# One decoder block with 32 experts on one core: the expert stage's tensor engine in written order, its gather and scatter products between weight chunks, and the first biases as three bfloat16 parts

## Chip, core and metric

The kernel runs on one NeuronCore of a Trainium2 chip. The metric is the device time of one execution in microseconds (us). Five engines work side by side: PE (TensorE: products and transposes, into PSUM), DVE (VectorE), ACT (ScalarE), POOL (GpSimd) and SP (SyncE, which here only issues transfers). PEld is PE's loading of the stationary operand. Sixteen DMA engines move data from HBM to the on-chip memory. A float32 product is recorded as two instructions, so a count in the trace is twice the count in the program for these.

## What is computed

A decoder block on 256 tokens of 1024 channels: a recurrent branch and an attention branch, merged and projected, a layer norm, and then a mixture of 32 experts of which each token uses 4, and a second layer norm. The change concerns the experts:

```python
def moe_ffn(x, router_w, router_b, expert_w_in, expert_b_in, expert_w_out, expert_b_out):
    ...
    logits = (xf @ router_w + router_b).astype(jnp.float32)
    top_val, top_idx = lax.top_k(logits, TOP_K)
    weights = jax.nn.softmax(top_val, axis=-1)
    ...
        h = xf[toks] @ expert_w_in[e] + expert_b_in[e]
        gate_h = jnp.minimum(h[:, :D_EXPERT], SWIGLU_LIMIT)
        lin_h = jnp.clip(h[:, D_EXPERT:], -SWIGLU_LIMIT, SWIGLU_LIMIT)
        act = gate_h * jax.nn.sigmoid(SWIGLU_ALPHA * gate_h) * (lin_h + 1.0)
        return act @ expert_w_out[e] + expert_b_out[e]
    ...
    out = jax.ops.segment_sum(ys * row_w[:, None].astype(ys.dtype), row_tok, num_segments=n_tok)
```

`expert_w_in[e]` is 1024 x 2048 and `expert_w_out[e]` 1024 x 1024, both float32: 12 MiB for each expert.

## The kernel before

The first part (branches, merge, projection, first norm, router) ends with `xg`, the rows of the first two experts' tokens. Everything after it is the expert stage. An expert has 64 slots (`CAP`) for its tokens. Experts go in pairs; a pair's 128 slots are filled together.

The weights come in 384 chunks of 1 MiB, twelve for each expert: eight for the first product (one for each 128 input channels) and four for the second. `stream` (line 770) issues their transfers from SP in the order of use, through `fetch`; they land in 21 places that are used in turn (`slots`, line 751: most are tiles named `ring`, some are pairs of halves named `wr`, `wh`/`wl`). A chunk can only be fetched into a place once PE has used the chunk that was there 21 chunks earlier.

The loop over `steps` (line 1365) writes for each expert e: `hidden` (products `h`, line 1254, after the bias products on line 1246), `swiglu` (DVE and ACT make `lc` out of `h`), `down` of expert e-1 (products `y`, line 1284), and `turned` (line 1273: `lc` transposed into `at`, which the next `down` reads). For each pair there are besides: `places` (DVE: the 0/1 matrix `oh` of the pair), `gather` (16 products `t<-oh,x`, line 1089, and eight evacuations by ACT and DVE into `xg`, line 1092), `weighted` and `scatter_weights` (two transposes of `oh`, line 1235, into `ct`), and `combine` (four products `t<-yp,ct`, line 1293, that DVE adds to `acc`, line 1297). `residual` and `spread` add the residual and the second biases, once each. Products of 64 slots use half of the array's columns, and the two halves of an expert's columns go one after the other on the two halves of the array.

Ahead of the expert stage a helper `queued` (line 122) fixes each engine's order as written. In the expert stage PE's instructions do not go through it: there the framework's scheduler sets the order, from its own estimates. The bias products of an expert take `expert_b_in` as float32 half rows on 64 partitions (`bin_`, the first 64 rows of the tile `biases`), with two columns of the identity as stationary operand; four products for each expert.

Before expert 16 stands `overflow()` (line 1299): each engine reads the largest number of tokens of an expert and branches; only if it is above 64 a slow loop runs, and in this data it does not. SP has then issued the first 21 chunks of expert 16 and what follows it.

Of the kernel before, what the change touches and what calls it, by code (L numbers as in the profile page):

```python
# [18 lines left out]
P = 128  # L19
# [15 lines left out]
# estimates, in us, of how long a step's other engines take before the tensor engine can go on with it:  # L35
# only the order in which work is traced rests on them
# [25 lines left out]
def shape_constants():  # L62
# [19 lines left out]
    # below the diagonal the level at which the two tokens' blocks merge; -0.5 on it, -1 above  # L82
# [15 lines left out]
def together(inputs):  # L98
    """small parameters, as rows of P of one array"""
# [12 lines left out]
def hybrid_block_kernel(ctx: ExitStack, tc: tile.TileContext, A, out):  # L112
# [5 lines left out]
    # instructions of one engine that follow each other as traced  # L118
# [17 lines left out]
    # slots of the experts' weights that hold other data first  # L136
# [8 lines left out]
    # halves of chunks: raw, and in two parts  # L145
# [30 lines left out]
    # the tensor engine's clock is up when the first data comes  # L176
# [6 lines left out]
    # ---- first loads  # L183
# [8 lines left out]
    def split(raw, n, engine):  # L192
        """hi and lo parts of half a chunk, rounded to float32r"""
# [24 lines left out]
    # the first products' data in small pieces  # L218
# [4 lines left out]
    # ---- small parameters  # L223
# [25 lines left out]
    # ---- the tensor engine's work, in the order in which it is traced  # L249
# [14 lines left out]
    # ---- x, with the channels on the partitions, in two parts  # L264
# [34 lines left out]
    def vectors():  # L299
# [4 lines left out]
        # sigmoid(z) is (1 + tanh(z / 2)) / 2, in the table that holds exp  # L304
# [7 lines left out]
    def three(ps, a, b, first, last, same_first=True):  # L312
        """ps += a^T b with a = (hi, lo), b = (hi, lo)."""
# [14 lines left out]
    def gemm_tm(w, ps, i):  # L328
        """[128 tokens, 2 blocks, 256 columns]"""
# [7 lines left out]
    # products of x with chunks of w_in: those that are asked for, else a gate's  # L337
# [40 lines left out]
    def shifted(ps, col, dst):  # L378
        """token shift: dst [128, 2, 256]."""
# [6 lines left out]
    # ---- low-rank inputs  # L386
# [13 lines left out]
    def rwkv_half(hf):  # L400
# [1111 lines left out]
```

## Time and profile before

| | us |
|---|---|
| median of 3 runs | 1300.01 (1298.52 to 1303.08) |
| span of the profiled execution | 1300.0 |
| expert stage (first `h` product to the end) | 299.6 to 1300.0 |

| engine | busy in the profiled execution |
|---|---|
| PE | 1225.3 us, 94% |
| DVE | 396.6 us, 31% |
| ACT | 263.2 us, 20% |
| POOL | 80.9 us, 6% |
| 16 DMA engines, main queue | 85.1% of their time |

The span leaves nothing of the time out, so sums can be made against it as it is. Busy shares are averages over stages of different kinds; the expert stage is read by stretches, and by who waits for whom. Matmul ends are modelled, so a PE that is shown busy is not PE at its peak: starts of groups are the better measure.

### The profile page before, as it was taken

What the parts mean: (1) busy time and instruction counts of PE and PEld (TensorE: products, weight loads), DVE (VectorE), ACT (ScalarE), POOL (GpSimd) and SP (SyncE); (2) the same over time, 40 slices, a digit from 0 to 9 for tenths busy, and PEclk for the clock granted to TensorE, in tenths of its full rate; (3) what the DMA queues carried; (4) which work ended last, traced back from release to release, by engine and by line L of the source; (5) the groups of instructions that cost most, each with busy time, mean ns of one, the idle gap of its engine ahead of it and who ended that gap; (6) DMA issues with size and microseconds to landing.
All of it is one profiled execution on the core that took longest, in us unless ns stands there. A gap on an engine that the chain in (4) does not pass through costs nothing. (4 is left out here: it accounts for less than half of the span.)

```text
span 1300.0 us, 15918 instructions
## 1 busy us (share of the span) xinstructions
PE 1225.3 (94%) x6524; PEld 593.2 (46%) x6524; DVE 396.6 (31%) x762; ACT 263.2 (20%) x486; POOL 80.9 (6%) x58
## 2 busy tenths in 40 slices
PE   9889989999999999999999998999999899999996
PEld 7778888974334332333323323334332323333433
DVE  6976762762123322111212201211112111111023
ACT  7456435542101010101101100101010101010111
POOL 2321221330000000000000000000000000000001
PEclk9989999999999999999999998999999999998899
DMA  8432442979999999999999997999999999999820
GB/s 271 147 102 95 176 163 101 327 275 376 412 416 413 415 415 415 412 405 410 406 413 373 412 417 318 410 418 414 414 416 413 416 412 416 416 415 403 339 97 33
DMA packets 114500, 439.32 MB, mean 338 GB/s; under 512 B 10062, under 2 KB 38552, under 8 KB 89592
## 3 DMA queue, kind: packets, MB, share of 16 engines
q1 hardware_dynamic: 113992, 437.94, 85.1%
q8 instruction: 53, 0.87, 0.3%
q10 hardware_dynamic: 432, 0.33, 0.1%
q14 instruction: 23, 0.19, 0.0%
HBM read 437.18 MB, written 1.05 MB: 337 GB/s over the span
## 5 line engine op out<-in xcount | busy, mean ns | idle before, releaser
L1254 PE MATMUL h<-ring,xg 128*64 128x512 f32 x1552 | 349.9, 598 | 0.0
L1254 PEld LDWEIGHTS h<-ring,xg 128*64 128x64 f32 x1552 | 108.7, 137 | 220.2 <-issue 209.6
L1284 PE MATMUL y<-ring,at 128*64 128x512 f32 x768 | 187.0, 619 | 1.9 <-ACT at L1275 1.9
L1262 DVE TENSOR_SCALAR h<-h 128x512 f32<-128x512 f32 x32 | 22.4, 699 | 399.6 <-PE h L1254 375.5
L1263 ACT ACTIVATE lc<-h 128x512 f32<-128x512 f32 x32 | 19.1, 597 | 492.7 <-DVE h L1262 433.0
L1246 PE MATMUL h<-biases,ident 64*64 64x512 f32 x256 | 93.1, 627 | 18.7 <-DVE lc L1266 13.3
L1284 PEld LDWEIGHTS y<-ring,at 128*64 128x64 f32 x768 | 53.6, 140 | 110.9 <-issue 103.5
L124 PE MATMUL g<-xh,wh 128*128 128x256 f32 x304 | 94.1, 310 | 2.6 <-DVE ring L384 1.9
L124 PE MATMUL g<-xh,wl 128*128 128x256 f32 x304 | 86.3, 284 | 1.5 <-DVE wl L199 1.5
L124 PE MATMUL g<-xl,wh 128*128 128x256 f32 x304 | 86.1, 283 | 0.0
L1297 DVE TENSOR_TENSOR acc<-acc,t 128x512 f32<-128x512 f32 x56 | 38.5, 687 | 140.8 <-PE t L1293 140.8
L1286 ACT COPY yp<-y 64x512 f32<-64x512 f32 x62 | 35.9, 579 | 210.6 <-PE y L1284 210.1
L1089 PEld LDWEIGHTS t<-oh,x 128*128 128x128 f32 x480 | 59.1, 197 | 26.0 <-issue 26.0
L124 POOL TENSOR_TENSOR acc<-acc,x 128x256 f32<-128x256 f32 x4 | 3.9, 994 | 1013.2 <-DVE ln_rs L124 1013.0
L1089 PE MATMUL t<-oh,x 128*128 128x128 f32 x480 | 66.2, 288 | 0.0
L124 PEld LDWEIGHTS g<-xh,wh 128*128 128x128 f32 x304 | 58.3, 192 | 11.9 <-issue 7.8
L1293 PE MATMUL t<-yp,ct 128*128 128x512 f32 x120 | 55.5, 605 | 6.8 <-ACT yp L1286 6.8
L124 PEld LDWEIGHTS g<-xl,wh 128*128 128x128 f32 x304 | 58.3, 192 | 2.2 <-issue 2.2
L124 PEld LDWEIGHTS g<-xh,wl 128*128 128x128 f32 x304 | 58.1, 191 | 1.9 <-DVE wl L199 1.7
L1092 DVE TENSOR_SCALAR xg<-t,gbc 128x128 f32<-128x128 f32 x60 | 24.6, 410 | 112.7 <-ACT xg L1092 112.7
L1246 PEld LDWEIGHTS h<-biases,ident 64*64 64x64 f32 x256 | 19.6, 135 | 76.2 <-issue 68.3
L1254 PE MATMUL h<-wr,xg 128*64 128x512 f32 x224 | 53.7, 597 | 0.0
(379 smaller groups left out, 1320.7 us busy)
## 6 DMA issues: line engine op xcount, KB each, us to landing
ring<-in_expert_w_in_dram SPq DMA_DIRECT2D x194, 1024.0 KB, 12.9
ring<-in_expert_w_out_dram SPq DMA_DIRECT2D x99, 1024.0 KB, 11.4
wr<-in_expert_w_in_dram SPq DMA_DIRECT2D x56, 512.0 KB, 13.5
wr<-in_w_in_dram SPq DMA_DIRECT2D x40, 512.0 KB, 3.8
wh<-in_expert_w_in_dram SPq DMA_DIRECT2D x34, 512.0 KB, 11.4
wl<-in_expert_w_in_dram SPq DMA_DIRECT2D x34, 512.0 KB, 11.4
wh<-in_expert_w_out_dram SPq DMA_DIRECT2D x20, 512.0 KB, 10.3
wl<-in_expert_w_out_dram SPq DMA_DIRECT2D x20, 512.0 KB, 10.2
```

The source lines that it names most:

```text
L124: queues[e] = make(*a, **k)
L1089: last = nc.tensor.matmul(ps[:, i * ns:(i + 1) * ns], lhsT=x1[:, b, k * P:(k + 1) * P], rhs=oh[:, b, :], start=b == 0 and i == 0, stop=b = ...
L1092: def scaled(ps, n, k0, put=lambda e, make, **a: make(**a)):
L1246: nc.tensor.matmul(h[half * CAP:(half + 1) * CAP, q, :], lhsT=sel_e[:, q:q + 1].to_broadcast([2 * E, CAP]), rhs=bin_[:, half * 512:(half + ...
L1254: nc.tensor.matmul(h[half * CAP:(half + 1) * CAP, q, :], lhsT=xg[:, k, sl], rhs=wi(k, c0), start=not early_bias and k == 0, stop=early_bia ...
L1262: nc.vector.tensor_scalar(out=gate_, in0=gate_, scalar1=7.0, scalar2=None, op0=ALU.min)
L1263: nc.scalar.activation(out=lc, in_=gate_, func=AF.Sigmoid, scale=1.702)
L1284: nc.tensor.matmul(y[dh * CAP:(dh + 1) * CAP, :], lhsT=at[:, kf % 4, kf // 4, :], rhs=wo_(kf, dh), start=kf == 0, stop=kf == KD - 1)
L1286: nc.scalar.copy(out=yp[r0_:r0_ + CAP, dh * 512:(dh + 1) * 512], in_=y[dh * CAP:(dh + 1) * CAP, :])
L1293: nc.tensor.matmul(ps, lhsT=ct[0:ns, b, :], rhs=yp[0:ns, hs], start=True, stop=True)
L1297: nc.vector.tensor_tensor(out=acc[:, b, hs], in0=acc[:, b, hs], in1=ps, op=ALU.add)
```

## The change

It does these things.

- **Order.** In the expert stage PE's instructions go through a wrapper `pe`, which is `queued("pe", ...)` except inside the overflow loop: PE runs them as written.
- **Where a pair's side work is written.** `gather` of the next pair comes whole after the odd expert's `hidden`, ahead of the `down` of the expert before. `combine` of a pair comes inside the `hidden` of the next pair's odd expert, after its second chunk. The transposes of `oh` come after the fourth chunk of the odd expert's `hidden`, `residual` in three pieces inside the `hidden` of experts 4 and 6, the four `spread` of the second norm inside that of expert 30.
- **First biases.** `expert_b_in` is fetched three times (32 rows each) by POOL into the memory of `acc`; DVE (first 1024 columns) and POOL (the others) split it into three bfloat16 parts that add up to the float32 value, on 96 partitions. A bias product then has one bfloat16 column of `own_rows` as stationary operand, and still there are four for each expert. The fetch of the float32 biases by SP ahead of the stage is gone.
- The transposed second-bias weights (`wtt`) live in the router's weights `rw` instead of a `ct`, and the second `started` pieces move by two chunks.

The diff, cut to its core (comment lines and renamed sites alike in kind are left out):

```diff
-    bin_ = biases[0:2 * E, :]
+    bin_ = biases[0:3 * E, :].bitcast(BF16)
...
+    own_rows = pers.tile([3 * E, E], BF16, name="own_rows")
+    for q in range(3):
+        qs = slice(q * E, (q + 1) * E)
+        nc.gpsimd.tensor_copy(out=own_rows[qs], in_=ident[qs, qs])
...
-            fetch(out=bin_, in_=L("expert_b_in").rearrange("e (h c) -> (e h) c", h=2))
...
+    raw_b = acc.rearrange("p b d -> p (b d)")[0:3 * E]
+    for q in range(3):
+        nc.gpsimd.dma_start(out=raw_b[q * E:(q + 1) * E], in_=L("expert_b_in"))
+    for eng, hs in ((nc.vector, slice(0, F)), (nc.gpsimd, slice(F, 2 * F))):
+        eng.tensor_copy(out=bin_[:, hs], in_=raw_b[:, hs])
+        for n in (2 * E, E):
+            eng.tensor_tensor(out=raw_b[0:n, hs], in0=raw_b[0:n, hs], in1=bin_[0:n, hs], op=ALU.subtract)
+            eng.tensor_copy(out=bin_[0:n, hs], in_=raw_b[0:n, hs])
+    free_order = [False]
+
+    def pe(make, *a, **k):
+
+        return make(*a, **k) if free_order[0] else queued("pe", make, *a, **k)
...
-                    nc.tensor.matmul(h[half * CAP:(half + 1) * CAP, q, :], lhsT=sel_e[:, q:q + 1].to_broadcast([2 * E, CAP]), rhs=bin_[:, half * 512:(half + 1) * 512], start=first, stop=not first)
+                    c0 = q * F + half * 512
+                    pe(nc.tensor.matmul, h[half * CAP:(half + 1) * CAP, q, :], lhsT=row.to_broadcast([3 * E, CAP]), rhs=bin_[:, c0:c0 + 512], start=first, stop=not first)
...
-                    nc.tensor.matmul(h[half * CAP:(half + 1) * CAP, q, :], lhsT=xg[:, k, sl], rhs=wi(k, c0), start=not early_bias and k == 0, stop=early_bias and k == KD - 1)
+                    pe(nc.tensor.matmul, h[half * CAP:(half + 1) * CAP, q, :], lhsT=xg[:, k, sl], rhs=wi(k, c0), start=not early_bias and k == 0, stop=early_bias and k == KD - 1)
+            for what in between.get(k, ()):
+                what()
...
+    extra = {}
+
+    def during(e, k, what):
+        extra.setdefault(e, {}).setdefault(k, []).append(what)
...
+    def gathered_(p):
+        p.xg = gather(p.oh, 2) if p.n else xg_t
+        p.ohw = weighted(p.oh, wt[:, :, 2 * p.n:2 * p.n + 2], 2) if p.n else None
...
+    for n, p in enumerate(pairs_of):
+        p.n = n
+        during(2 * n + 1, 3, lambda p=p: turned_weights(p))
+        if n < E // 2 - 1 and 2 * n + 2 != E // 2:
+            during(2 * n + 3, 1, lambda p=p: combined(p))
+            during(2 * n + 1, 3, lambda p=pairs_of[n + 1]: placed(p))
+    for j in range(2):
+        r = residual(j)
+        for k in (4, 5, 7):
+            during(4 + 2 * j, k, lambda r=r: next(r, None))
+    during(0, 5, softmax)
...
+            h = hidden(p.xg, slice(i * CAP, (i + 1) * CAP), lambda k, c0: part(c[k], c0, 512), own_rows[:, e:e + 1], e > 1, extra.get(e, {}))
+            if i and e < E - 1 and e + 1 != E // 2:
+                gathered_(pairs_of[e // 2 + 1])
             lc = swiglu(h)
```

PE around experts 8 to 10, before: expert 9's `h`, then expert 8's `y`. (`t<-ident,lc` is `turned`, `t<-oh,x` a gather, `t<-ident,oh` the transposes of `oh`, `t<-yp,ct` a combine.)

```order
L1254 MATMUL h<-ring,xg 64x512 x8
L1235 MATMUL t<-ident,oh 128x128 x2
L1254 MATMUL h<-ring,xg 64x512 x24
L1284 MATMUL y<-ring,at 64x512 x4
L1273 MATMUL t<-ident,lc 128x128 x4
L1089 MATMUL t<-oh,x_121 128x128 x2
L1284 MATMUL y<-ring,at 64x512 x4
L1089 MATMUL t<-oh,x_121 128x128 x6
```

The same place after the change (line 124 is `queued`):

```order
L124 MATMUL h<-ring,xg 64x512 x8
L124 MATMUL t<-yp,ct 128x512 x4
L124 MATMUL h<-ring,xg 64x512 x8
L124 MATMUL t<-ident,oh 128x128 x2
L124 MATMUL h<-ring,xg 64x512 x16
L1094 MATMUL t<-oh,x_121 128x128 x16
L124 MATMUL y<-ring,at 64x512 x16
L124 MATMUL t<-ident,lc 128x128 x4
L124 LDWEIGHTS own_rows
L124 MATMUL h<-biases,own_rows 64x512
```

`turned` of expert 9 stood after a quarter of expert 8's `y`, and now stands after all of it; the gather stood in pieces inside `y` and now stands whole ahead of it; the combine of the pair before moved in between the chunks of expert 9.

PE at the start of the stage, before (expert 0's last products, its biases, then expert 1):

```order
L1254 MATMUL h<-ring,xg 64x512 x32
L1246 MATMUL h<-biases,ident 64x512 x4
L1216 LDWEIGHTS ones
L1216 MATMUL t<-mk,ones 128x32
L1216 LDWEIGHTS ones
L1216 MATMUL t<-mk,ones 128x32
L1254 MATMUL h<-ring,xg 64x512 x11
L1273 MATMUL t<-ident,lc 128x128 x4
```

After, from the last of expert 0's four bias products on:

```order
L124 LDWEIGHTS own_rows
L124 MATMUL h<-biases,own_rows 64x512
L124 MATMUL t<-ident,lc 128x128 x4
L124 MATMUL h<-ring,xg 64x512 x16
L124 MATMUL t<-ident,oh 128x128 x2
```

`turned` of expert 0 moved ahead of all products of expert 1.

DVE at the same place, before, from the last `weighted` of the first pair to expert 0's `swiglu`:

```order
L1163 TENSOR_TENSOR oh<-oh,wt 128x128
L1262 TENSOR_SCALAR h<-h 128x512
L1217 TENSOR_REDUCE cnt<-t 1x1
L1218 CAST cnt_i<-cnt 1x1
L1264 TENSOR_SCALAR h<-h 128x512
```

And after:

```order
L1168 TENSOR_TENSOR oh<-oh,wt 128x128
L1188 CAST biases<-acc 96x1024
L1190 TENSOR_TENSOR acc<-acc,biases 64x1024
L1191 CAST biases<-acc 64x1024
L1190 TENSOR_TENSOR acc<-acc,biases 32x1024
L1240 TENSOR_REDUCE cnt<-t 1x1
L1191 CAST biases<-acc 32x1024
L1241 CAST cnt_i<-cnt 1x1
L1288 TENSOR_SCALAR h<-h 128x512
```

The five steps of the split on DVE now stand between them; POOL has five like them, behind its three transfers.

## Rows read from the trace of the kernel before

**Rows 1.** The profile page: in 40 equal slices of the span (32.5 us each) the mean busy share of the DMA engines in tenths and what they moved.
```profile
DMA  8432442979999999999999997999999999999820
GB/s 271 147 102 95 176 163 101 327 275 376 412 416 413 415 415 415 412 405 410 406 413 373 412 417 318 410 418 414 414 416 413 416 412 416 416 415 403 339 97 33
```

**Rows 2.** Stretches of the expert stage: start and end, length, busy us of PE, PEld, DVE, ACT and POOL (instructions in brackets), granted PE clock as a share of 2.4 GHz, DMA share, GB/s.
```profile
325.00:500.00 175.00, 173.87 (x799) 65.36 (x796) 43.15 (x79) 18.85 (x35) 0.00 (x0) 1.00 1.02 414
500.00:775.00 275.00, 257.51 (x1143) 91.19 (x1143) 49.90 (x91) 28.68 (x53) 0.00 (x0) 0.99 1.01 406
...
925.00:1200.00 275.00, 258.49 (x1120) 89.52 (x1118) 46.91 (x89) 26.55 (x50) 0.00 (x0) 0.98 1.02 414
...
1245.00:1290.00 45.00, 40.24 (x231) 18.12 (x230) 9.07 (x18) 5.34 (x10) 0.00 (x0) 1.00 0.00 1
325.00:1247.00 922.00, 879.13 (x3917) 322.16 (x3914) 178.83 (x332) 98.53 (x183) 0.00 (x0) 0.98 1.00 404
```

**Rows 3.** What SP, the issuer of the transfers, waited for between 325 and 1247 us: total us, times, longest. Line 124 is `queued`, line 1302 the branch of `overflow`.
```profile
SPq L124 <- PE h L1254: 317.2, 211, 10.5
SPq L124 <- PE y L1284: 134.6, 79, 6.8
...
SPq L1302 <- SPq L1302: 14.5, 3, 9.7
```

**Rows 4.** Groups of instructions by line between 500 and 1200 us: PE's weight loads for `h` out of `ring`, with the idle time ahead of them and what ended it.
```profile
L1254 PEld LDWEIGHTS h<-ring,xg 128*64 128x64 f32 x1096 | 76.3, 137 | 153.5 <-issue 147.0 <-ACT xg L1092 5.7 <-DMA ring<-in_expert_w_out_dram 0.3
```

**Rows 5.** PE's timeline (start, length of the merged group, in us) over one pair of experts, 18 and 19, from one gather to the next.
```profile
838.15 3.74 PE L1089 MATMUL t<-oh,x 128*128 128x128 f32 x32
841.82 1.93 PE L1246 MATMUL h<-biases,ident 64*64 64x512 f32 x8
843.68 13.95 PE L1254 MATMUL h<-ring,xg 128*64 128x512 f32 x64
...
864.43 1.07 PE L1246 MATMUL h<-biases,ident 64*64 64x512 f32 x2
865.43 3.70 PE L1293 MATMUL t<-yp,ct 128*128 128x512 f32 x8
...
869.50 1.93 PE L1246 MATMUL h<-biases,ident 64*64 64x512 f32 x6
871.35 3.65 PE L1254 MATMUL h<-wr,xg 128*64 128x512 f32 x16
...
893.12 3.74 PE L1089 MATMUL t<-oh,x 128*128 128x128 f32 x32
```

**Rows 6.** PE's timeline in the projection ahead of the stage: products of one pass over 512 columns (`wh`, `wl`, `mh` are float32 rounded to one pass), one after the other.
```profile
268.03 0.40 PE L124 MATMUL w<-wh,mh 128*128 128x512 f32 x1
268.26 0.40 PE L124 MATMUL w<-wl,mh 128*128 128x512 f32 x1
```

**Rows 7.** Timelines of PE and DVE after expert 9's `h`: expert 8's `y`, the `turned` that waits for `lc` (idle time ahead of it in brackets), and the last step of `swiglu` that it waits for.
```profile
577.24 1.89 PE L1284 MATMUL y<-ring,at 128*64 128x512 f32 x8
581.02 0.66 PE L1273 MATMUL t<-ident,lc 128*128 128x128 f32 x4 [1.89 <-DVE lc L1266]
```
```profile
577.45 0.70 DVE L1262 TENSOR_SCALAR h<-h 128x512 f32<-128x512 f32 x1 [9.74 <-PE h L1254]
580.27 0.69 DVE L1266 SCALAR_TENSOR_TENSOR lc<-h,lc 128x512 f32<-128x512 f32 x1
```

**Rows 8.** The start of the stage: PE's timeline (the router's last products, expert 0's biases, expert 1's first `h`), DVE's last step ahead of expert 0's `swiglu`, the groups of 1024-column operations on DVE and POOL (busy us, mean ns of one), and the time to landing (minimum, median, maximum, us) of the transfers into `ring` between 40 and 160 us.
```profile
293.21 1.21 PE L1041 MATMUL a<-rw,m 128*128 128x32 f32 x8 [0.73 <-ACT m L124]
...
313.50 1.93 PE L1246 MATMUL h<-biases,ident 64*64 64x512 f32 x8
...
315.52 5.36 PE L1254 MATMUL h<-ring,xg 128*64 128x512 f32 x22
```
```profile
305.07 0.29 DVE L1163 TENSOR_TENSOR oh<-oh,wt 128x128 f32<-128x128 f32 x1
```
```profile
L124 DVE TENSOR_TENSOR wl<-wr,wh 128x1024 fp32r<-128x1024 f32 x4 | 4.9, 1226 | 2.5 <-ACT wh L124 2.5
```
```profile
L124 POOL TENSOR_TENSOR wl<-wr,wh 128x1024 fp32r<-128x1024 f32 x4 | 9.8, 2443 | 31.2 <-ACT wh L124 31.2
```
```profile
DMA to landing us min/median/max: 5.8/5.9/7.8
```

**Rows 9.** Around the branch: PE's timeline from the last combine ahead of it to expert 16's first `h`, and short stretches with the columns of rows 2.
```profile
780.42 3.70 PE L1293 MATMUL t<-yp,ct 128*128 128x512 f32 x8 [0.68 <-ACT yp L1286]
789.47 1.94 PE L1246 MATMUL h<-biases,ident 64*64 64x512 f32 x2 [5.34 <-PEq L1302]
...
799.05 4.51 PE L1254 MATMUL h<-ring,xg 128*64 128x512 f32 x20
```
```profile
798.00:800.00 2.00, 2.00 (x10) 0.51 (x9) 0.68 (x2) 0.46 (x1) 0.00 (x0) 1.00 0.00 0
800.00:802.00 2.00, 2.00 (x12) 0.68 (x10) 0.00 (x0) 0.00 (x0) 0.00 (x0) 1.00 0.00 0
```

**Rows 10.** PE's timeline at the end: the products of the very last chunk.
```profile
1286.78 1.97 PE L124 MATMUL t<-ring,at 128*64 128x128 f32 x32
```

**Rows 11.** A fall of PE's clock: PE's timeline with an idle time in brackets, and the stretch behind it with the columns of rows 2.
```profile
674.66 1.04 PE L1246 MATMUL h<-biases,ident 64*64 64x512 f32 x2 [1.99 <-DVE lc L1266]
```
```profile
676.00:680.00 4.00, 4.00 (x12) 0.90 (x9) 0.00 (x0) 0.00 (x0) 0.00 (x0) 0.57 1.03 426
```

More of the change, by code (lines that the diff above doesn't have):

```diff
@@ L1200, in residual @@
             nc.vector.scalar_tensor_tensor(out=acc[:, b, hs], in0=t, scalar=ALPHA, in1=acc[:, b, hs], op0=ALU.mult, op1=ALU.add)
+        yield
+        for b in range(NB):
             ps = mwork()
-            nc.tensor.matmul(ps, lhsT=wtt[:, b, :], rhs=bo[:, hs], start=True, stop=True)
+            pe(nc.tensor.matmul, ps, lhsT=wtt[:, b, :], rhs=bo[:, hs], start=True, stop=True)
             nc.vector.tensor_tensor(out=acc[:, b, hs], in0=acc[:, b, hs], in1=ps, op=ALU.add)
@@ L1280, in down @@
         for kf in range(KD):
-            if last and kf in (2, 4):
-                started(kf // 2 - 1)
+            if last and kf in (4, 6):
+                started(kf // 2 - 2)
             for dh in range(2):
-                nc.tensor.matmul(y[dh * CAP:(dh + 1) * CAP, :], lhsT=at[:, kf % 4, kf // 4, :], rhs=wo_(kf, dh), start=kf == 0, stop=kf == KD - 1)
+                pe(nc.tensor.matmul, y[dh * CAP:(dh + 1) * CAP, :], lhsT=at[:, kf % 4, kf // 4, :], rhs=wo_(kf, dh), start=kf == 0, stop=kf == KD - 1)
         for dh in range(2):
@@ L1350, in last_done, with placed, turned_weights, combined @@
                 queued("act", nc.scalar.copy, out=dst, in_=src)
+    extra = {}
+    def during(e, k, what):
+        extra.setdefault(e, {}).setdefault(k, []).append(what)
+    class Pair:
+        pass
+    pairs_of = [Pair() for _ in range(E // 2)]
+    def placed(p):
+        p.oh = places(r1[:, :, 2 * p.n:2 * p.n + 2], 2) if p.n else oh_t
+    def gathered_(p):
+        p.xg = gather(p.oh, 2) if p.n else xg_t
+        p.ohw = weighted(p.oh, wt[:, :, 2 * p.n:2 * p.n + 2], 2) if p.n else None
+    def turned_weights(p):
+        if p.n == 0:
+            p.ohw = weighted(p.oh, wt[:, :, 0:2], 2)
+        p.ct = scatter_weights(p.ohw, 2, "")
+    def combined(p):
+        combine(p.ct, p.yp, P, p.n == 0)
+    for n, p in enumerate(pairs_of):
[9 more added lines that the diff above has]
+    during(0, 5, softmax)
+    gb2 = x1.rearrange("p b d -> p (b d)")
+    for q in range(4):
+        during(E - 2, 2 * q, lambda q=q: nc.scalar.copy(out=gb2[:, q * 512:(q + 1) * 512], in_=spread(4 + q)))
+    placed(pairs_of[0])
+    gathered_(pairs_of[0])
     for kind, e in steps:
         i = e % 2
+        p = pairs_of[e // 2]
         c0 = first_of[kind, e]
@@ L1358, in hybrid_block_kernel @@
                 overflow()
-            if i == 0:
-                es = slice(e, e + 2)
-                if e:
-                    oh = places(r1[:, :, es], 2)
-                    xg = gather(oh, 2)
-                else:
-                    xg = xg_t
-            if e == E - 2:
-                gb2 = x1.rearrange("p b d -> p (b d)")
-                for q in range(4):
-                    nc.scalar.copy(out=gb2[:, q * 512:(q + 1) * 512], in_=spread(4 + q))
+                placed(p)
+                gathered_(p)
             stream(c0 + KD)
             c = tiles[c0:c0 + KD]
-            h = hidden(xg, slice(i * CAP, (i + 1) * CAP), lambda k, c0: part(c[k], c0, 512), ident[0:2 * E, 2 * e:2 * e + 2], e > 1)
-            if e == 0:
-                softmax()
-            if i == 0:
-                ohw = weighted(oh, wt[:, :, es], 2)
-            if e in (3, 5):
-                residual((e - 3) // 2)
+            h = hidden(p.xg, slice(i * CAP, (i + 1) * CAP), lambda k, c0: part(c[k], c0, 512), own_rows[:, e:e + 1], e > 1, extra.get(e, {}))
+            if i and e < E - 1 and e + 1 != E // 2:
+                gathered_(pairs_of[e // 2 + 1])
             lc = swiglu(h)
```

35 lines of the change are left out of this document (19 added, 16 removed).

## The prediction

> **What bounds the kernel now.** I read the slices of the page first, then stretches of the expert stage, then who waits for whom. The slices show the transfers at 410 to 418 GB/s from slice 11 to the end but for a few dips, and a tail of about two slices in which almost nothing lands [rows 1]. So two limits lie close together: the DMA engines, which read about 414 GB/s at their best over long stretches with a busy share of 1.02, and PE, which is shown busy nearly all of the time [rows 2]. Which of the two leads is settled by the waits. SP, which fetches the weights, waited 317.2 us for `h` and 134.6 us for `y`, that is, for PE to free a place, 452 of the 922 us between 325 and 1247 [rows 3]. PE's weight loads for `h` waited 0.3 us for a transfer in 700 us [rows 4]. And after the last weights have landed, near 1246, PE still works 40 of the next 45 us [rows 2]. PE is behind by the whole store of 21 chunks, all of the time, to the end. The stage is PE's, with the DMA engines just below it.
>
> How far below: an expert has 12 chunks of 1.0486 MB, 12.58 MB; at 414 GB/s that is 30.4 us. Between 500 and 775 it moved 406 GB/s, one expert in 31.0 us [rows 2]. PE without waits does better: the pair 18 and 19 takes 893.12 - 838.15 = 54.97 us, 27.5 us for each [rows 5]. The other 3.5 us are waits and work in pieces: PE sat idle 275 - 257.5 = 17.5 us in that stretch, 2.0 for each of its 8.9 experts [rows 2], and a typical one is `turned`, which stands after a quarter of `y` and waits 1.89 us for DVE's `lc` [rows 7].
>
> **The biases.** In that pair they take 1.86 us (841.82 to 843.68), 1.00 (864.43 to 865.43) and 1.85 (869.50 to 871.35), 4.71 in all [rows 5]. Afterwards there are eight products of one pass over 512 columns. One such product after another costs 0.23 us [rows 6], so 1.84 us is the upper bound. The `h` products go in twos on the two halves of the array: 64 records of two passes in 13.95 us, 0.109 us for a pass [rows 5], so 0.87 us is the lower one. These are the same shape in output and place as `h`, so I take 0.9. The pair falls to 54.97 - 4.71 + 0.9 = 51.2 us, 25.6 for each expert.
>
> **The order.** Nothing is removed; work changes its place, and what counts is the cover. `lc` is ready 580.27 + 0.69 - 577.24 = 3.7 us after the last `h` [rows 7]. In the new order `turned` comes after all of `y`: 32 records at `h`'s rate are 7.0 us, and after odd experts the gather of 3.74 us [rows 5] lies ahead of that as well. So DVE's and ACT's chain is covered with 3.3 us to spare, and evacuating the gather has the 7.0 us of `y`. If that cover is gone, the old wait of about 1.9 us is back. The combine needs `yp`, which ACT copies behind `y`; it now has `turned`, the biases and two chunks (3.5 us) as cover. DVE's four sums and the two transposes of `oh` come between chunks and delay only PE, by what they cost before. So PE should need 25.6 us for an expert, at worst what it needs now less 1.9, about 29.1. Both are below 30.4.
>
> **What is late next** is the stream of weights. From 325 to 1247 us the DMA engines moved 922 x 404 GB/s = 372.5 MB [rows 2]. At 414 GB/s that takes 899.7 us, and ends at 1224.7 if nothing holds it up. PE gains 30.4 - 25.6 = 4.8 us on it with each expert; the store holds 21 chunks, 53 us, so PE has caught up after about 11 of the first 16 experts and waits for chunks from there on.
>
> **The branch.** Before, the last combine ends at 784.1, PE waits to 789.47, and the first `h` of expert 16 comes at 799.05 [rows 9]; the transfers run dry, with 0 GB/s from 798 to 802 [rows 9]. Two things end there: SP's own 14.5 us at the branch [rows 3], in which the transfers that it has issued land, and the first place that expert 16 frees. A PE that has caught up reaches the branch when expert 15's last chunk has landed, 21 chunks (53 us) before SP's last one does, so its own 15 us lie beside transfers. SP's running dry stays. It costs between 0 and the 5.5 us or so of before; I take 3.
>
> **The start.** The float32 biases can be fetched when the router's last product ends, at 294.4 [rows 8]. The trace has no transfer issued by POOL. In a quiet stretch SP's took 5.8 to 7.8 us to land [rows 8]; three in a row may take twice that, so 300 to 310. DVE's five steps at 1.23 us take 6.1 us and lie in its idle time from 305.36 on; POOL's five at 2.44 us take 12.2 [rows 8]. The parts are there between 312 and 322; PE wants them at 313.5 [rows 8]. Then `turned` of expert 0 stands ahead of all of expert 1 and waits the 3.7 us of `lc` in the open. Expert 1 starts at 313.5 + 0.5 + 3.7 + 0.6 = 318.3 at the earliest, 2.8 us later than before, and up to 11 later. For the stream only a part counts, since the slice there moved 376 of 414 GB/s [rows 1]; I take 1.5, bounds 0 and 9. The extra bytes (0.8 MB now, 0.26 MB less earlier, 1.3 us of DMA time) fit into that same room. POOL's three small casts for `own_rows` fall where POOL idles; under 1 us either way.
>
> **The tail.** The last chunk comes in two pieces. Once the second has landed PE owes half of the last 1.97 us [rows 10], 1.0, and then what followed that group: 1300.0 - 1288.75 = 11.25 us. For landing, hand-over and a PE at the lower clock I add 1.5 (0 to 3).
>
> **Sum**, made against the profiled span of 1300.0, which is the median: 325 + 899.7 + 3 + 1.5 + 12.25 + 1.5 = 1243.0 us. Two thirds of what is gained is the 40 us and more of PE's arrears at the end, the rest the dips of the stream.
>
> **Rivals.**
> - *The written order makes PE wait.* A fixed order cannot fill a hole with other work. The stream hides waits up to 30.4 - 25.6 = 4.8 us for each expert; beyond it each microsecond costs 29 (the experts after the start). With 6 us of waits PE needs 31.6, and the end is 1243 + 29 x 1.2 = 1278. For it: the 1.89 us waits are real [rows 7]. Against it: they came where cover was a quarter of `y`, and 2.0 us for each expert was all idle time there was [rows 2].
> - *The clock falls while PE waits for chunks, and the kernel gets slower.* After an idle time of 1.99 us PE ran at 0.57 of its clock between 676 and 680, partly at 1.2 GHz [rows 11]. Once PE has caught up it waits, on the mean, 4.8 / 12 = 0.4 us for each chunk. A share f of PE's work at half the clock makes 25.6 (1 + f) us of an expert. The stream covers that to f = 0.19; at 0.27 (32.5 us) the end is 1243 + 29 x 2.1 = 1304, slower than now; at 0.4 it is 1243 + 29 x 5.4 = 1400. Against it: between 500 and 775 PE idled 17.5 us and the mean clock was 0.99, and with no idle time it was 1.00 [rows 2], so a PE that falls behind stops waiting and gets its clock back. The Trainium skill ("TensorE: Matmul & The Clock Gate", section "HAM oscillation — how this bites in real kernels") describes a kernel whose PE waits for DMA between short bursts of products, falls back to the low clock at each wait and starts each burst cold; if that carried over, this rival would be the forecast. The trace agrees that waits bring the clock down, but only after waits of near 2 us, five times the mean wait expected here.
> - *It does not do what it says:* the stream was the limit already and PE's time is free. Then 1300. The waits [rows 3, 4] and the 40 us behind the last landing [rows 2] speak against it.
>
> **How the numbers follow.** The forecast has 0.84, with its own range 1234 (stream at 418, no losses) to 1258 (start 9, branch 5.5, tail 3, stream at 412). The waiting order has 0.07, the clock 0.04, no effect 0.03; 0.02 is left for a faster end. The range 1234 to 1262 takes in the unknown costs and the lighter part of the first rival. About 0.3%, 4 us, is what a measurement can tell from no change. Faster by more: 0.92; within it: 0.04 (no effect, and a waiting order that just cancels the biases); slower: 0.04.
>
> **What would show it.** Right: SP's waits for PE nearly gone and waits for its own earlier transfers in their place; PE's loads of `h` waiting for DMA; 414 GB/s from slice 11 to the last weights, with one short dip at the branch; 12 to 14 us from the last weights to the end; bias products below 0.5 us for an expert. Wrong: PE waiting for `lc` or `xg` in the second half of the stage, a granted clock well below 0.95 there, a gap of more than 10 us ahead of expert 1, or PE still working through a store of chunks after the last landing.

## The result, and the profile after

| | before | after |
|---|---|---|
| median of 5 runs, us | 1298.82 (1291.66 to 1303.08) | 1260.99 (1254.38 to 1264.57) |
| ratio, 95% interval | | 0.9708 (0.9667 to 0.9748) |
| profiled execution: span, us | 1300.0 | 1252.3 (its time 1254.38) |

The forecast was 1243.0, with a range of 1234 to 1262. The change makes the kernel 2.9% faster, by the mechanism of the forecast, and falls short of the forecast's size: the median went down by 38 us where 57 were forecast. It lies 1 us inside the range, and two of the five executions (1263.78 and 1264.57) lie above it, so the range held only just. The forecast was made in spans, and a span is shorter than the time of its execution (1252.3 and 1254.38 here): against times it stands some 2 us too low. The profiled execution is the fastest of the five; what sets it apart from the median comes at the end.

The profile page, DMA share and GB/s in 40 slices of 31.3 us (before: [rows 1]):

```profile
DMA  8433355688999999999999999899999999999995
GB/s 277 146 95 119 100 186 171 221 322 311 373 415 412 416 413 417 415 414 415 412 417 414 414 415 414 346 412 416 415 414 416 413 416 412 416 414 415 416 413 190
```

The tail of two slices without transfers is gone, and of the dips one is left (346, slice 26). Stretches of the stage, with the columns of [rows 2]:

```profile
325.00:500.00 175.00, 175.00 (x850) 68.23 (x848) 44.83 (x84) 19.56 (x36) 0.00 (x0) 1.00 1.01 408
500.00:775.00 275.00, 253.16 (x1190) 94.33 (x1186) 51.45 (x99) 31.42 (x58) 0.00 (x0) 0.99 1.02 415
...
925.00:1200.00 275.00, 253.94 (x1197) 92.24 (x1198) 48.87 (x96) 33.90 (x62) 0.00 (x0) 1.00 1.02 415
```

What SP waited for between 325 and 1247 us ([rows 3]: 317.2 us for `h`, 134.6 for `y`), and what PE waited for in the same time:

```profile
SPq L124 <- DMA ring<-in_expert_w_in_dram: 248.1, 131, 3.3
SPq L124 <- DMA ring<-in_expert_w_out_dram: 173.3, 83, 2.8
SPq L124 <- PE h L124: 94.2, 69, 13.0
...
SPq L124 <- PE y L124: 22.9, 28, 5.4
```
```profile
PE t L124 <- DVE lc L1292: 26.2, 1, 26.2
PE y L124 <- DMA ring<-in_expert_w_out_dram: 19.0, 29, 1.5
PE h L124 <- DMA ring<-in_expert_w_in_dram: 15.0, 22, 1.5
PE t L1094 <- DVE oh L1080: 5.6, 1, 5.6
```

The roles have changed: SP's waits for PE to free places are down from 452 to 117 us, it now waits mainly for its own earlier transfers, and PE waits for chunks, in pieces of at most 1.5 us. Two waits are out of line, both near the branch: 26.2 us in a single piece, and before it 5.6 us for the `oh` of the pair of expert 16, whose gather starts at 755.30. PE's timeline over experts 18 and 19 ([rows 5] is the same pair):

```profile
830.13 0.62 PE L124 MATMUL h<-biases,own_rows 96*64 96x512 bf16 x4
830.58 13.90 PE L124 MATMUL h<-ring,xg 128*64 128x512 f32 x64
...
851.87 0.62 PE L124 MATMUL h<-biases,own_rows 96*64 96x512 bf16 x4
852.32 3.60 PE L124 MATMUL h<-wr,xg 128*64 128x512 f32 x16
...
881.83 0.41 PE L124 MATMUL h<-biases,own_rows 96*64 96x512 bf16 x2
```

The pair takes 881.83 - 830.13 = 51.70 us, 25.85 for an expert (27.5 before), and the biases 0.45 us each time, start to start.

To compare executions, the stage is cut at transfers whose landing the trace records. Chunk 31, the last weights of expert 1, is the first that feels the whole start; the last piece of all weights ends the stream. All in us, one profiled execution each, and each worked out as a difference of two times in the trace. The start is the same code in after, after_again, no_branch, own_tile and tail, and chunk 31 lands there 38.2 to 40.2 us behind the first `h`: differences of up to 2 us in that column can be chance.

| kernel | first `h` at | first `h` to landing of chunk 31 | chunk 31 to last landing | last landing to end | first `h` to end |
|---|---|---|---|---|---|
| before | 299.6 | 33.2 | 913.3 | 53.9 | 1000.4 |
| after | 297.7 | 40.0 | 898.3 | 16.3 | 954.6 |
| after_again | 301.5 | 40.2 | 898.6 | 16.2 | 955.0 |
| start_cover | 302.3 | 36.3 | 898.4 | 16.3 | 951.0 |
| dve_parts | 305.7 | 36.5 | 898.2 | 16.2 | 951.0 |
| no_branch | 304.4 | 39.3 | 895.2 | 16.4 | 951.0 |
| own_tile | 295.8 | 39.2 | 899.0 | 16.3 | 954.5 |
| tail | 304.4 | 38.2 | 898.3 | 15.8 | 952.4 |
| bias_only | 300.2 | 37.0 | 898.1 | 20.9 | 956.0 |
| order_only | 304.2 | 35.3 | 899.3 | 16.1 | 950.7 |
| pad11 | 305.4 | 37.5 | 917.5 | 54.3 | 1009.3 |
| best | 301.3 | 35.4 | 899.0 | 15.1 | 949.4 |
| best_f32 | 303.8 | 33.3 | 898.3 | 15.0 | 946.5 |

The third column of times is the finding in one look: with PE anywhere from 25.85 to 27.31 us for an expert (order_only: 27.31, half of the 54.62 us from the gather at 824.58 to the one at 879.20), the stream takes 898 to 899 us with the branch and 895 without it.

### The profile page after: what moved, and what is told of

The parts are those of the page before. It is cut to its first block, busy times and chain, and to the rows that moved or that the text cites. A ratio compares the mean times of both kernels' runs of the same rounds, so it can differ in the third digit from the quotient of the medians.

```text
span 1252.3 us, 15684 instructions
## 1 busy us (share of the span) xinstructions
PE 1145.6 (91%) x6396; PEld 570.4 (46%) x6396; DVE 401.0 (32%) x767; ACT 264.3 (21%) x486; POOL 94.1 (8%) x69
## 5 line engine op out<-in xcount | busy, mean ns | idle before, releaser
L124 PE MATMUL h<-ring,xg 128*64 128x512 f32 x1552 | 353.9, 599 | 15.4 <-DMA ring<-in_expert_w_in_dram 15.0
L124 PE MATMUL y<-ring,at 128*64 128x512 f32 x768 | 177.0, 598 | 20.3 <-DMA ring<-in_expert_w_out_dram 19.0
L1094 PE MATMUL t<-oh,x 128*128 128x128 f32 x480 | 58.9, 282 | 5.6 <-DVE oh L1080 5.6
L1094 PEld LDWEIGHTS t<-oh,x 128*128 128x128 f32 x480 | 56.1, 196 | 17.3 <-issue 17.3
L124 PE MATMUL t<-yp,ct 128*128 128x512 f32 (+1 forms) x124 | 56.5, 598 | 0.7 <-ACT yp L1312 0.7
L199 POOL TENSOR_TENSOR wl<-wr,wh 128x1024 fp32r<-128x1024 f32 x18 | 44.0, 2443 | 133.9 <-ACT wh L198 123.5
L198 ACT CAST wh<-wr 128x1024 fp32r<-128x1024 f32 (+1 forms) x44 | 42.1, 970 | 39.9 <-PE g L124 27.9
L124 PE MATMUL t<-ident,lc 128*128 128x128 f32 x128 | 21.9, 296 | 29.8 <-DVE lc L1292 29.8
## 6 DMA issues: line engine op xcount, KB each, us to landing
wr<-in_expert_w_in_dram SPq DMA_DIRECT2D x56, 512.0 KB, 16.3
```

What stands on the lines that cost most here:

```text
L124: queues[e] = make(*a, **k)
L198: nc.scalar.copy(out=hi[:, sl], in_=raw[:, sl])
L199: engine.tensor_tensor(out=lo[:, sl], in0=raw[:, sl], in1=hi[:, sl].bitcast(F32), op=ALU.subtract)
L1094: last = nc.tensor.matmul(ps[:, i * ns:(i + 1) * ns], lhsT=x1[:, b, k * P:(k + 1) * P], rhs=oh[:, b, :], start=b == 0 and i == 0, stop=b = ...
```

## Experiments: the floor

**bias_only.** The bfloat16 bias parts in the kernel before, nothing else:

```diff
-    bin_ = biases[0:2 * E, :]
+    bin_ = biases[0:3 * E, :].bitcast(BF16)
...
-                    nc.tensor.matmul(h[half * CAP:(half + 1) * CAP, q, :], lhsT=sel_e[:, q:q + 1].to_broadcast([2 * E, CAP]), rhs=bin_[:, half * 512:(half + 1) * 512], start=first, stop=not first)
+                    nc.tensor.matmul(h[half * CAP:(half + 1) * CAP, q, :], lhsT=row.to_broadcast([3 * E, CAP]), rhs=bin_[:, q * F + half * 512:q * F + half * 512 + 512], start=first, stop=not first)
...
```

> The kernel before with the three bfloat16 bias parts alone; PE's order in the expert stage is the scheduler's, as before. Theory (the stream of weights is a floor near 1252 us, and either part of the change alone brings PE under it): PE's own 30 experts are 1.9 us shorter each, 1300 - 57 + 5 for the start = 1248, so close to the floor that the store is not quite worked off: 1255 to 1268 us. Rival (the two parts add up to the 40 us, each with its share): 1275 to 1285.

**order_only.** The written order with the float32 biases of before (what the change does to the biases undone: parts, `own_rows` and POOL's transfers).

> The changed kernel with the float32 biases of before (four products over 64 partitions, fetched by SP ahead of the stage), so that the written order is alone. Theory (the floor of the stream): PE needs 25.85 + 1.9 = 27.75 us for an expert, still under the stream's 30.4, and works off the 35.8 us of store that it has after the branch in 13 experts; there is no wait for bias parts at the start, so the time is that of the changed kernel less 3 to 7 us, 1246 to 1256 us. Rival (the parts add up): 1270 to 1285, with PE still behind the last landing.

Measured: bias_only 1259.98 us, ratio 0.9716 (0.9681 to 0.9752); order_only 1260.70, ratio 0.9726 (0.9693 to 0.9759). Each half alone gives all but a few tenths of a per cent of what both give (0.9708), so the gains don't add. order_only's 1260.70 lies 5 us above its expected interval, though in its profile it is 950.7 us from the first `h` to the end, 4 less than after: its first `h` came late, at 304.2. PE takes 27.31 us for an expert there, less than the 27.75 that was expected. With bias_only PE works off its store less well and the tail is 20.9 us long.

**fewer_bytes and pad11.** Two tests from both sides of the floor: fewer transfers at the same work, and more work at the same transfers.

```diff
-            views += [ewo[e, :, 2 * q:2 * q + 2, :] for q in range(4)]
+            views += [ewo[e, :, 2 * q:2 * q + 2, :] for q in range(3)]
```
```diff
         if early_bias:
-            biases_(True)
+            for i in range(11):
+                biases_(i == 0, False)
```

> The changed kernel with eleven chunks for an expert: it leaves out the transfer of the fourth chunk of the second product of all experts but the last, and PE multiplies by the third chunk twice instead, so that PE's work is the same. Theory (the transfers are the bound): 31 chunks less at 2.53 us are 78 us, of which PE, at 25.85 us for an expert against 27.9 for eleven chunks, leaves some 74: about 1180 us (1172 to 1190), with PE now almost at its own limit. Rival (PE's order or its clock is the bound): within 20 us of the changed kernel.

> The changed kernel with the bias products of experts 2 to 31 run eleven times (the bias is added eleven times), 4.5 us more of PE's work for each expert: 25.85 + 4.5 = 30.35 us, as much as the stream's 30.4. Theory (PE has to be clearly under the stream to work off its store of 21 chunks, 53 us, by the end): it stays behind by the store, and the end comes as in the kernel before behind the last landing, at 1295 to 1315 us. Rival (whatever is under the stream's 30.4 is free): 1254 to 1264 us.

fewer_bytes: 1186.38 us, ratio 0.9145 (0.9118 to 0.9171), 74.6 us less than the changed kernel at the median. pad11: 1316.87 us, ratio 1.017 (1.0116 to 1.0224), just above its expected interval. Here is PE with fewer bytes in the second half, and what SP waited for under pad11:

```profile
900.00:1150.00 250.00, 249.53 (x1199) 95.49 (x1196) 52.32 (x97) 32.87 (x59) 0.00 (x0) 1.00 1.02 415
```
```profile
SPq L124 <- PE h L124: 442.3, 251, 12.1
SPq L124 <- PE y L124: 153.3, 101, 5.4
```

With eleven chunks PE has no idle time left (249.53 of 250 us): 25.85 us for an expert against 11 x 2.541 = 27.95 for its chunks (2.541 us for a chunk is worked out further on) is too little room to work off the store, and the end comes 20.6 us behind the last landing. So the room between the two limits was as small as expected. With more on PE the profile of before is back, SP waiting for `h` and 54.3 us of work behind the last landing, although an expert takes PE 30.17 us there (half of the 60.34 from the gather at 852.7 to the one at 913.1), less than the 30.49 of twelve chunks. PE must be under the stream by enough to work off its store of 21 chunks, not merely level with it.

## Experiments: start, branch, tail

**start_cover.** Work is put into PE's wait ahead of expert 1 (`hidden` of expert 0 hands its bias products on in `late_bias`):

```diff
+    def first_lc():
+        late_bias[0]()
+        h_first.append(swiglu(h_first.pop()))
+    during(1, 2, first_lc)
+    during(1, 6, lambda: h_first.append(turned(h_first.pop())))
```

> The changed kernel, except that the bias products of expert 0 come after the third chunk of expert 1's `h`, and `turned` of expert 0 after its seventh, so that PE has work while the bias parts are made and while DVE and ACT make `lc`. Theory (the start cost is the stream's: SP could not free a place while PE stood before expert 1, from 311.9 to 322.3): expert 1 starts near 312, the issue that waited until 325.4 comes near 315, chunk 31 lands near 334.5 instead of 337.7, and the kernel ends about 3 us earlier (1 to 6). Rival (the store of 21 chunks hides whatever PE does at the start): same time, and the later landings are where they were.

**dve_parts.** The bias parts without POOL:

```diff
-    for eng, hs in ((nc.vector, slice(0, F)), (nc.gpsimd, slice(F, 2 * F))):
+    for eng, hs in ((nc.vector, slice(0, F)), (nc.vector, slice(F, 2 * F))):
```

> The changed kernel with all bias parts made by DVE, first for one half of the columns, then for the other; POOL makes none. Theory (DVE and POOL held each other up: each of DVE's later casts ended 0.5 us after a subtraction of POOL, at 2.50 us, where the first cast took 0.69): alone, DVE casts in 0.7 us each and subtracts in 1.1 to 1.3, ten steps in 8.5 to 9.5 us instead of the 10.6 that both together took (306.3 to 316.9), and expert 1 starts some 1 to 2 us earlier behind the first `h` than the 24.6 of the changed kernel. Rival (the later casts are slow in themselves, for their 64 or 32 partitions): 2.5 us each again, 16 us in all, and expert 1 starts 5 us later.

The start of the changed kernel on PE, DVE and POOL:

```profile
316.07 0.64 PE L124 MATMUL h<-biases,own_rows 96*64 96x512 bf16 x2 [4.15 <-DVE biases L1191]
316.97 0.64 PE L124 MATMUL h<-biases,own_rows 96*64 96x512 bf16 x2 [0.26 <-POOL biases L1191]
321.21 1.12 PE L124 MATMUL t<-ident,lc 128*128 128x128 f32 x4 [3.60 <-DVE lc L1292]
322.26 8.26 PE L124 MATMUL h<-ring,xg 128*64 128x512 f32 x32
```
```profile
306.32 0.69 DVE L1188 CAST biases<-acc 96x1024 bf16<-96x1024 f32 x1 [2.90 <-DMA acc<-in_expert_b_in_dram]
307.05 1.94 DVE L1190 TENSOR_TENSOR acc<-acc,biases 64x1024 f32<-64x1024 f32 x1
309.02 2.51 DVE L1191 CAST biases<-acc 64x1024 bf16<-64x1024 f32 x1
```
```profile
308.00 2.99 POOL L1190 TENSOR_TENSOR acc<-acc,biases 64x1024 f32<-64x1024 f32 x1
311.05 1.38 POOL L1191 CAST biases<-acc 64x1024 bf16<-64x1024 f32 x1
```

PE waits 4.15 us for the parts and 3.60 for `lc`, with nothing else to do. DVE's cast from 309.02 to 311.53 ends 0.5 us after POOL's subtraction (308.00 to 310.99). With POOL left out (dve_parts, operations on `biases`: nanoseconds min/median/max, first and last start in us):

```profile
L1190 DVE TENSOR_TENSOR acc<-acc,biases x4: 1206/1208/1209, 314.5 to 319.1; 64x1024 f32<-64x1024 f32 x2, 32x1024 f32<-32x1024 f32 x2
L1191 DVE CAST biases<-acc x4: 673/675/677, 316.7 to 320.8; 64x1024 bf16<-64x1024 f32 x2, 32x1024 bf16<-32x1024 f32 x2
```

The same cast takes 0.675 us instead of 2.51, the subtraction 1.21 instead of 1.94, and DVE alone makes all parts in 8.2 us (313.24 to 321.47), faster than both engines together (10.6). Expert 1 starts 20.8 us behind the first `h` instead of 24.6, more than was expected; 1.1 of these 3.7 us come from the transfers, which landed that much earlier. The rival, that these casts are slow in themselves, is out. Both kernels land chunk 31 some 3.5 us earlier (36.3 and 36.5 instead of 40.0), as the first theory of start_cover had it; that the store hides all of the start is out as well. It hides a part: in start_cover expert 1 starts 10.5 us earlier than in after (14.1 us behind the first `h`), in dve_parts 3.7, and both gain about the same. Times: start_cover 1253.37 us, ratio 0.9642 (0.9600 to 0.9683); dve_parts 1258.46, ratio 0.9664 (0.9631 to 0.9697). In start_cover the theory's times for the first places were off: its first `h` came 4.6 us later than after's, and expert 1 at 316.4 rather than near 312; as distances from the first `h` they hold (14.1 us to expert 1, 36.3 to chunk 31).

**no_branch** and **own_tile.** The first leaves `overflow()` out; the second moves the place into which the loop behind the branch fetches:

```diff
-                    t = moe.tile([P, 512], F32, name="lc")
-                    nc.sync.dma_start(out=t, in_=src[bass.ds(ev, 1), :, k, c0:c0 + 512].rearrange("e p c -> (e p) c"))
+                    t = rw.rearrange("p k e -> p (k e)")
+                    nc.sync.dma_start(out=t, in_=src[bass.ds(ev, 1), :, k, c0:c0 + 256].rearrange("e p c -> (e p) c"))
...
```

> The changed kernel without the overflow branch ahead of expert 16: it leaves out the loop for experts with more than 64 tokens, which this data never enters. Theory (the stream of weights is the bound, and the branch costs it only the time in which nothing lands): PE's 26.2 us of idle time after expert 16's `h` is gone, the dip from 795 to 800 is gone, and the time falls by about 3 us (2 to 5). Rival (PE's idle time at the branch counts in full or in part): 10 to 26 us less.

> The changed kernel, except that the loop behind the branch (not entered with this data) fetches its weight pieces, now 256 columns wide, into the router's weights `rw` instead of `lc`. Theory on the 26.2 us of idle time (ACT's first `lc` after the branch waits until SP, which is the one that fetches into `lc` in the loop, has passed the branch): ACT no longer waits for SP there, PE goes on after some 4 us. Theory on the time (PE's idle time there is covered by the stream): the dip of the stream at the branch stays, 3 us long, and the span from the first `h` to the end stays within 1 us of 955. Rival (PE's idle time counts): 10 us less or more. Rival on the wait (it is not `lc`'s place that ties ACT to SP): PE's idle time stays at 26 us.

The 26.2 us, in the changed kernel: ACT's timeline, then PE's, around the branch (idle time in brackets with what ended it; line 1329 is the branch):

```profile
798.14 0.60 ACT L1289 ACTIVATE lc<-h 128x512 f32<-128x512 f32 x1 [36.17 <-SPq L1329]
```
```profile
800.97 1.11 PE L124 MATMUL t<-ident,lc 128*128 128x128 f32 x4 [26.21 <-DVE lc L1292]
```

And PE in own_tile, with the stretch in which the stream runs dry there (columns of [rows 2]):

```profile
780.71 0.66 PE L124 MATMUL t<-ident,lc 128*128 128x128 f32 x4 [3.62 <-DVE lc L1298]
```
```profile
790.00:795.00 5.00, 5.00 (x26) 1.69 (x24) 0.82 (x3) 0.00 (x0) 0.00 (x0) 1.00 0.42 172
795.00:800.00 5.00, 5.00 (x33) 2.92 (x30) 1.40 (x2) 0.65 (x2) 0.00 (x0) 1.00 0.59 190
```

PE's wait shrinks from 26.2 to 3.6 us, and the time from the first `h` to the end stays at 954.5 (after: 954.6). So the wait came from `lc`: SP would write it in the loop, and ACT's next write of `lc` waits until SP has passed the branch, though the loop is not entered. And the 22 us of PE's time were free. Without the branch the stream is 3.1 us shorter (895.2 instead of 898.3), not 10 to 26. Times: no_branch 1253.50 us, 0.9629 (0.9583 to 0.9675); own_tile 1258.93, 0.9693 (0.9653 to 0.9732).

**tail** and the measure for these sets, **after_again**:

```diff
-            if last and kf in (4, 6):
-                started(kf // 2 - 2)
+            if last and kf == 6:
+                started(1)
...
+    def first_sums():
+        z = ph.tile([P, 2, 512], F32, name="h")
+        zs.append([z[:, b, :] for b in range(NB)])
+        started(0)
+    during(E - 1, 5, first_sums)
```

> The changed kernel, except that the first of the three groups of `acc` products that start the last sums stands inside expert 31's `h` (after its sixth chunk, in the PSUM place of expert 30's `h`) instead of between the chunks of expert 30's `y`. Theory (behind the last `y` of expert 30 PE is late by work that could have been done earlier; 2.9 us lie between the last landing and the products that use it): PE reaches the last chunk's products 1.5 us earlier and the end comes 1 to 2 us earlier. Rival (the tail follows from the last landing alone): the end does not move.

> The changed kernel once more, as the measure for the other three of this set: 1254 to 1264 us, its ratio to the kernel before between 0.966 and 0.975, the landing of chunk 31 near 338 and the last landing 16 us ahead of the end in its profile.

after_again: 1257.95 us, 0.9672 (0.9620 to 0.9724); tail: 1259.28, 0.9685 (0.9642 to 0.9727). In the time nothing can be told. In the profile PE begins the last chunk's products 1.7 us after the last landing instead of 2.9, so PE was late there, but only 0.4 of these 1.2 us reach the end (15.8 instead of 16.3): the sums now share one PSUM tile, and a sum waits for the statistics of its neighbour (0.53 us). The rest of tail's 2.2 us from the first `h` to the end lies at the start (38.2 instead of 40.0), which the edit does not touch.

**best** and **best_f32.** All that helped, with the sums put ahead of their statistics and the third chunk's products into the wait for `yp`:

```diff
+    down_last(at, c[2], y[:, 256:384], range(KD), P)
+    last_done(y[:, 256:384], 512, P, yp, CAP)
-    gathered(0, 0)
-    measured(0, 0)
-    down_last(at, c[2], y[:, 256:384], range(KD), P)
-    last_done(y[:, 256:384], 512, P, yp, CAP)
-    gathered(0, 1)
-    measured(0, 1)
+    for b in range(NB):
+        gathered(0, b)
+    for b in range(NB):
+        measured(0, b)
```

> The changed kernel with the start covered (bias products of expert 0 and its `turned` inside expert 1's `h`), the loop's pieces in `rw`, and the tail drawn together (the first `acc` products inside expert 31's `h`; the products of the last expert's third chunk ahead of the first two sums, so that they stand in the wait for `yp`; both sums ahead of their statistics). Theory: 3.7 us less at the start, nothing at the branch, 2.2 at the tail; 949 us from the first `h` to the end instead of 955, ratio to the kernel before 0.960 to 0.965, and 4 to 7 us under the changed kernel. Rival (one of them gives its gain back further on): the span from the first `h` to the end stays above 951.

> The same kernel with the float32 biases of before, fetched by SP ahead of the stage: no transfers by POOL at the start, but 1.9 us more of PE for each expert. Theory (PE's time is free as long as it works off its store before the end): with no idle time at the branch PE's 27.75 us are enough, and without 0.8 MB of transfers by POOL at the start chunk 31 lands 33 to 34 us after the first `h` instead of 36.3: 946 us from the first `h` to the end, some 3 us under the kernel with bfloat16 parts. Rival (PE's room is needed at the end): 950 or more, with PE still behind when the last chunk lands.

From the first `h` to the end they take 949.4 and 946.5 us, expected 949 and 946. The times are 1252.66 us, 0.9650 (0.9614 to 0.9686), and 1257.05, 0.9677 (0.9637 to 0.9717): against the changed kernel (0.9672 and 0.9708 in its two sets) the intervals overlap, so that these 5 to 8 us are shown by one profile each and not by the times.

## Why the prediction was right, and where its size was off

**What bounds the kernel, and that the stream comes next: right.** Both views that named PE as late ([rows 3] and the work behind the last landing in [rows 2]) turned over as foreseen, and fewer_bytes and pad11 show from both sides that the transfers are the limit now.

**The cost of each part on PE: right.** Biases 0.90 us for a pair (forecast 0.9), an expert 25.85 (25.6). PE meets the stream at expert 12 (forecast: after about 11). There is no wait for `xg`, and none for `lc` but the one at the branch, so the first rival fell; order_only, with PE at 27.31 us, shows how much room it would have had.

**The clock rival: wrong here.** Between 925 and 1200 us PE waits for chunk after chunk, up to 1.5 us each, and the granted clock is 1.00. It falls at longer waits, to 0.50, the 1.2 GHz level: in the 26.2 us at the branch, for a few us about the 5.6 us before it, and at the start, behind the 4.15 us that PE waits for the bias parts. Stretches at the start and at the branch, with the columns of [rows 2]:

```profile
315.00:320.00 5.00, 1.28 (x4) 0.26 (x3) 2.74 (x5) 0.60 (x1) 1.85 (x2) 0.50 1.01 421
```
```profile
780.00:785.00 5.00, 0.00 (x0) 0.00 (x0) 0.00 (x0) 0.00 (x0) 0.00 (x0) 0.50 1.02 409
805.00:810.00 5.00, 5.00 (x24) 1.49 (x22) 0.00 (x0) 0.00 (x0) 0.00 (x0) 0.91 1.02 429
```

At the start it is not free: `turned` takes 1.12 us instead of 0.66, and the first 32 records of expert 1's `h` 8.26 instead of some 7.0 (64 records take 13.90). The rival was nearer than after's trace shows: in own_tile one wait of 1.69 us for a chunk brought the clock down as well (0.50 from 1055.1 to 1058.5), though no time is seen to be lost by it (954.5 us from the first `h` to the end). The Trainium skill ("TensorE: Matmul & The Clock Gate", section "HAM oscillation — how this bites in real kernels") tells of a kernel that falls back at each wait for data, with waits of about 3 to 5 us; the trace agrees for the waits of 4.15, 5.6 and 26.2 us, and the shorter ones of this kernel are not that case.

**The sum.** To compare term by term I set the forecast's terms out from before's landing of chunk 31, 332.8: they give a last landing at 332.8 + 1.5 + 352 x 1.0486 MB / 414 GB/s + 3 = 1228.8 (the forecast's own sum has 1229.2) and 13.75 us of tail, 1242.6 in all. Against that the profiled execution (1252.3) has:

- first `h` at 297.7 instead of 299.6: -1.9
- the start, 6.8 us (40.0 - 33.2) instead of 1.5: +5.3
- the stream, 898.3 instead of 894.5: +3.8. Chunk 31 to chunk 211 come every 2.541 us ((795.1 - 337.7) / 180), 412.7 GB/s, a little less than the 414 of the forecast. That is 2.9. The last five chunks take 13.8 us instead of 12.7: 1.1. The branch takes 2.8 instead of 3
- the tail, 16.3 instead of 13.75: +2.5

1242.6 + 9.7 = 1252.3. **The start is the mis-sized term.** Its steps were foreseen one by one (transfers landing, ten operations, then 3.7 us of `lc` in the open), within the bound of 9, but two sizes failed. "DVE's five steps at 1.23 us take 6.1 us": next to POOL they took 9.7. The Trainium skill ("SBUF — State Buffer", section "Who interferes with whom") says that DVE and GpSimd share a pair of ports, and that the one that has it blocks the other for a whole instruction; the trace agrees (2.51 us next to POOL, 0.675 alone). And "For the stream only a part counts", at 1.5 us: only a part did count, but most of it. Expert 1 started 24.6 us behind the first `h` instead of 15.9 (322.26 and 315.52 in the two traces), 8.7 us later, and 6.8 reached the stream. The last of these microseconds count nearly in full (dve_parts starts expert 1 3.7 us earlier and gains 3.5), and before that there is slack: start_cover starts it 10.5 us earlier and gains no more than 3.7 of the 6.8. The other 2 to 3 us (36.3 in start_cover and 35.4 in best against 33.3 in best_f32, 33.2 before) remain although expert 1 starts earlier there than in before, and go when the bias parts go altogether. That points to fetching them, which no run isolates, and it is little more than the spread of that column: POOL's three transfers took 19.9% of the 16 DMA engines' time between 296 and 312 us, 3.2 us, and between 300 and 305 the engines, busy all of the time, moved 233 GB/s.

**The branch: right number, wrong picture.** The run-dry of 3 us is confirmed by no_branch (3.1). That a PE that has caught up loses nothing there was wrong: it stood for 26.2 us, since ACT was tied to SP. It cost nothing only because the stream covers it; own_tile shows both.

**The tail.** PE's timeline at its end:

```profile
1228.77 1.03 PE L124 MATMUL t<-acc,ident 128*128 128x256 f32 x4
1230.29 3.67 PE L124 MATMUL t<-ring,at 128*64 128x256 f32 x32 [0.49 <-ACT at L1301]
1234.89 1.12 PE L124 MATMUL z<-yp,ct 128*128 128x512 f32 x2 [0.93 <-DVE yp L124]
...
1238.89 1.97 PE L124 MATMUL t<-ring,at 128*64 128x128 f32 x32
```

"Once the second piece has landed PE owes half of the last 1.97 us" took PE as idle at the last landing (1236.0). It reached these products at 1238.89: from 1219.7 on it stands for ACT (0.49 us) and DVE (0.93) and for no transfer, so the chain of `y`, `turned`, `at` and sums behind the last `h` is the compute engines' own, not the stream's.

**From profile to median.** The median misses the forecast by 18.0 us: 9.3 are the terms above (1252.3 - 1243.0), 2.1 the time outside the span, and 6.6 the distance from the profiled execution's time (1254.38) to the median. The forecast had no term for the last two, and it is luck that its range held in spite of them. after_again shows a difference of that kind in a trace: its stage is the same (955.0), its first `h` comes 3.8 us later. Stretches of the first part, in after and in after_again:

```profile
200.00:210.00 10.00, 10.00 (x101) 9.05 (x98) 3.78 (x13) 5.14 (x14) 0.00 (x0) 1.00 0.39 124
```
```profile
200.00:210.00 10.00, 10.00 (x90) 9.37 (x90) 1.66 (x8) 2.90 (x9) 0.00 (x0) 0.50 0.06 21
```

In the second PE runs at 0.50 of its clock, from 193.7 to 210.7, while it is busy. Of the 14 traces (fewer_bytes included), nine have a mean clock of 0.83 between 190 and 240 us, with PE busy all of the 50 us, and their first `h` comes at 300.2 to 305.7. The other five have 0.97 to 1.00 there, and first `h` at 295.8 (own_tile), 297.7 (after), 299.2, 299.6 and 304.2 (order_only). So the fall goes with a late first `h`, but order_only is late without it. What starts the fall, and whether it accounts for the spread of the runs that have no trace, stays open.

## What to carry to other kernels

When two limits lie close together, lowering one of them buys only the distance to the other, and the parts of a change do not add: price each part against the second limit, alone. A delay of the engine that frees buffers can cost the stream at the start (here 6.8 us, of a start 8.7 us later), when the issuer has nothing else to fetch into, while 22 us of it at the branch cost nothing; so look at the first microseconds of a stage with more care than at its middle. Compare executions from a mark inside the program (here the first `h`): the spans of best and best_f32 from there to the end, 949 and 946 us, were foreseen and found to within 1, while the whole times could not tell them apart.

## What the runs showed of the hardware

- A bfloat16 cast of 64 x 1024 on DVE took 0.675 us alone and 2.51 next to a subtraction on POOL; ten operations were done sooner by one engine (8.2 us) than by two (10.6).
- Three transfers of 0.26 MB issued by POOL took 3.2 us of all 16 DMA engines, 0.79 MB / 3.2 us = 247 GB/s, where SP's weights run at 412.7.
- A branch whose loop is not entered still made ACT wait 36.2 us for SP, because the loop would fetch into a tile that ACT writes next.
- PE's clock fell to 0.50 for some microseconds between 190 and 240 us in nine of 14 traces (mean clock 0.83) and not in after (1.00), with PE busy 50.00 of 50 us in both.
- Waits of up to 1.5 us for chunks left PE's clock at 1.00 (after, 925 to 1200 us); waits of 1.69 (own_tile), 4.15, 5.6 and 26.2 us were each followed or accompanied by 0.50, and one of 1.89 in before ([rows 7]) was not.
